# Strassen's seven products for part of the block pairs of the gates, mix_out and the down projection

## The chip, the cores and the metric

The kernel runs on one core of a Trainium2 chip. The metric is device time in microseconds (us): the median of three executions. One execution was recorded by the hardware profiler, and every row below comes from that one.

## The reference

One decoder layer for 256 tokens of width 2048, in float32. What matters here:

- `h = rms_norm(x)`, and `h @ w_in` gives q, k, v, the three inputs of a short convolution (1024 wide each) and two gates `ga`, `gc` (2048 wide each).
- `merged = sigmoid(ga) * (attention @ w_attn_out) + sigmoid(gc) * (convolution @ w_conv_out)`, and then `x = x + merged @ w_mix_out`.
- cross-attention to 256 memory tokens (`wkv_x`, `wq_x`, `wo_x`), and `u = relu(rms_norm(x) @ w_up)`, `x + (u * u) @ w_down` with a hidden width of 8192.
- a last `rms_norm`.

## The kernel before

**Three matmuls for each product.** Every matrix product runs as a sum of three in the type float32r: each operand is split into a high part (a copy rounded to float32r) and a low part (the rest), and hi x hi, hi x lo and lo x hi are added up in PSUM. The activations lie with the features on the partitions. Weights come from HBM in tiles of two 128-row blocks by 512 columns (512 KB, `load_w`, L58 on SP's queue, pool `wraw`, 6 buffers). `split_w` makes the high part on ScalarE (L66) and the low part on VectorE (L67), in pool `wsp`, 5 buffers each.

**Token groups.** `tok_group(w, c0, kr0, nk, xs, evac)` computes 512 columns for all 256 tokens: two PSUM banks, one for each half of the tokens, and for each of the nk 128-deep blocks and each half three 128x512 matmuls (L103 to L105). When a half is done, `evac` takes it out of PSUM. The up projection uses `feat_group` instead (L78 to L82), which puts its result by features.

**Stages in order.** q, k and v with the first group written out apart (it splits `x` and the weights as they land); self-attention and convolution, interleaved; then for each of four column blocks the two gates (L332 to L334, nk = 16, taken out by a ScalarE sigmoid straight from PSUM, L333), `w_attn_out` and `w_conv_out` (nk = 8, L337 to L342), and four pairs of transposes that put the merged block by features (`mg`); mix_out in four groups (L350 on, residual sum L355, sum of squares L189, transposes and `split_scaled`, L134 and L135, with `memory` for the memory tokens in between); cross-attention; and four times a quarter of the MLP, four up groups and four down groups (nk = 16, L459 adds to the residual). The last column block of the last down group is cut into half-width pieces, so that the end comes in small steps (L466, L510 to L520).

**Order of instructions.** The program text gives priorities; a scheduler at compile time lays out every engine's instructions by them and by a cost model of its own, so work written later can run earlier where its inputs are there by that model. Each engine then runs its own list strictly in order. The raw tile of `x` by tokens, `xtok`, is loaded at the start on ScalarE's DMA queue (L246), and the eight sums of squares for the first norm are ScalarE's (L189).

**PSUM.** Eight banks: five for accumulators (`mm`), three for transposes and attention (`aux`).

## Time and profile before

| what | value |
|---|---|
| median of 3 executions | 1476.53 us (1476.36 to 1476.88) |
| the profiled execution | 1476.77 us, span 1475.0 us |
| mean granted TensorE clock | 0.996 of 2.4 GHz |
| TensorE matmul busy | 1454.8 us (99%), 7064 matmuls |
| VectorE busy / ScalarE busy | 820.9 us (56%) / 691.2 us (47%) |
| HBM read | 277.98 MB, 190 GB/s over the span |

The span runs from the first to the last instruction; 1.77 us of the execution's time lie outside it. Busy times are unions of the records of an engine. A matmul's record is longer than the distance to the next one, since matmuls are pipelined, so TensorE's pace is read from start to start. The same holds in a smaller measure of VectorE and ScalarE.

### The profile page before, as it was taken

The page shows a single profiled execution, that of the slowest core. Times are in us where ns is not written, and L with a number is a line of the kernel's source. Part 1 is how long each engine was busy: PE and PEld are TensorE (multiplying, and loading weights), DVE is VectorE, ACT ScalarE, POOL GpSimd, SP SyncE. Part 2 cuts the span into 40 slices and gives each one's busy share as a digit, 9 for nine tenths or more (in the row PEclk, how much of TensorE's full clock was granted, in tenths as well). Part 3 has the DMA queues.
Part 4 walks back from the last instruction along what each step waited for, and adds up shares of the span by engine and source line. Part 5 has one row for each costly group of instructions (what it writes and reads, how often), then busy time and mean ns, then how long its engine had stood idle before and what let it go on. Part 6 is the DMA issues. An engine that isn't in the chain of part 4 may idle for free.

```text
span 1475.0 us, 18233 instructions
## 1 busy us (share of the span) xinstructions
PE 1454.8 (99%) x7064; PEld 1222.4 (83%) x7064; DVE 820.9 (56%) x976; ACT 691.2 (47%) x905; POOL 13.6 (1%) x21
## 2 busy tenths in 40 slices
PE   6999999999999999999999999999999999999997
PEld 5888888888888888888888888888888888888886
DVE  5545555765554646654476655556545555556554
ACT  6444544454444445554564443444434443445442
POOL 0000000000000000000000000000000000000011
PEclk9999999999999999999999999999999999999999
DMA  9666655576666667655555566565565556665652
GB/s 337 193 193 180 184 165 178 170 227 190 187 196 188 186 197 230 212 192 180 172 171 185 187 198 191 182 197 180 194 200 179 193 188 191 192 191 179 198 189 85
DMA packets 145158, 281.27 MB, mean 191 GB/s; under 512 B 8880, under 2 KB 9520, under 8 KB 144944
## 3 DMA queue, kind: packets, MB, share of 16 engines
q1 hardware_dynamic: 141888, 272.66, 58.9%
q10 hardware_dynamic: 3184, 7.45, 1.5%
q8 instruction: 55, 0.90, 0.2%
q14 instruction: 31, 0.25, 0.1%
HBM read 277.98 MB, written 2.10 MB: 190 GB/s over the span
## 4 chain that ended last, share of the span: by engine, by line
PE 98%; DMA 1%; ACT 1%; issue 0%; DVE 0%; POOLq 0%; POOL 0%; DVEq 0%; SPq 0%; ACTq 0%
PE acc L104 23%; PE acc L105 23%; PE acc L103 23%; PE acc L78 15%; PE acc L79 8%; PE aps L145 1%; PE acc L82 1%; DMA tok<-in_x_dram 1%; PE acc L81 1%; DMA raw<-in_w_in_dram 0%; ACT junk L189 0%; PE aps L315 0%; PE aps L270 0%; PE aps L438 0%; PE aps L407 0%
## 5 line engine op out<-in xcount | busy, mean ns | idle before, releaser
L67 DVE TENSOR_TENSOR wlo<-raw,whi 128x1024 fp32r<-128x1024 f32 (+1 forms) x510 | 618.7, 1222 | 561.2 <-ACT whi L66 547.5
L66 ACT ACTIVATE whi<-raw 128x1024 fp32r<-128x1024 f32 (+1 forms) x510 | 532.9, 1055 | 564.1 <-PE acc L105 386.2
L103 PE MATMUL acc<-whi,S 128*128 128x512 f32 x1512 | 584.9, 388 | 11.4 <-ACT whi L66 11.4
L105 PE MATMUL acc<-whi,S 128*128 128x512 f32 x1512 | 587.9, 389 | 0.0
L104 PE MATMUL acc<-wlo,S 128*128 128x512 f32 x1512 | 586.3, 388 | 0.3 <-DVE wlo L67 0.3
L103 PEld LDWEIGHTS acc<-whi,S 128*128 128x128 f32 x1512 | 284.6, 188 | 68.8 <-ACT whi L66 12.7
L78 PE MATMUL acc<-S,whi 128*128 128x512 f32 x960 | 341.6, 398 | 0.0
L104 PEld LDWEIGHTS acc<-wlo,S 128*128 128x128 f32 x1512 | 284.5, 188 | 58.8 <-DVE wlo L67 1.6
L105 PEld LDWEIGHTS acc<-whi,S 128*128 128x128 f32 x1512 | 284.7, 188 | 56.2
L79 PE MATMUL acc<-S,wlo 128*128 128x256 f32 x960 | 269.7, 281 | 0.0
L78 PEld LDWEIGHTS acc<-S,whi 128*128 128x128 f32 x960 | 180.4, 188 | 41.3
L79 PEld LDWEIGHTS acc<-S,wlo 128*128 128x128 f32 x960 | 181.3, 189 | 3.1
L474 ACT ACTIVATE blk<-acc 128x256 f32<-128x256 f32 x64 | 24.3, 380 | 36.0 <-PE acc L82 35.8
L189 ACT ACTIVATE junk<-tok 128x512 f32<-128x512 f32 (+1 forms) x33 | 20.2, 613 | 37.7 <-DVE tok L459 23.6
L459 DVE SCALAR_TENSOR_TENSOR tok<-acc,q,tok 128x512 f32<-128x512 f32 (+1 forms) x33 | 24.1, 731 | 18.0 <-PE acc L105 18.0
L130 ACT ACTIVATE S<-blk 128x512 fp32r<-128x512 f32 x32 | 20.0, 626 | 25.7 <-DVE blk L478 25.7
L475 DVE TENSOR_TENSOR blk<-acc,blk 128x256 f32<-128x256 f32 x64 | 27.0, 422 | 8.0 <-ACT blk L474 8.0
L131 DVE TENSOR_TENSOR S<-blk,S 128x512 fp32r<-128x512 f32 x32 | 22.1, 692 | 9.9 <-ACT S L130 8.4
L82 PE MATMUL acc<-S,whi 128*128 128x512 f32 x64 | 25.6, 400 | 0.0
L478 DVE SCALAR_TENSOR_TENSOR blk<-blk 128x512 f32<-128x512 f32 x32 | 22.0, 689 | 0.6
L204 ACT ACTIVATE blk<-acc,r 128x512 f32<-128x512 f32 x18 | 12.4, 689 | 15.5 <-PE acc L105 15.5
L81 PE MATMUL acc<-S,wlo 128*128 128x256 f32 x64 | 18.1, 283 | 0.0
(127 smaller groups left out, 466.2 us busy)
## 6 DMA issues: line engine op xcount, KB each, us to landing
raw<-in_w_in_dram SPq DMA_DIRECT2D x158, 512.0 KB, 4.2
raw<-in_w_up_dram SPq DMA_DIRECT2D x128, 512.0 KB, 4.0
raw<-in_w_down_dram SPq DMA_DIRECT2D x128, 512.0 KB, 4.3
raw<-in_w_mix_out_dram SPq DMA_DIRECT2D x32, 512.0 KB, 4.9
raw<-in_w_attn_out_dram SPq DMA_DIRECT2D x16, 512.0 KB, 4.3
raw<-in_w_conv_out_dram SPq DMA_DIRECT2D x16, 512.0 KB, 4.5
raw<-in_wkv_x_dram SPq DMA_DIRECT2D x16, 512.0 KB, 4.2
raw<-in_wq_x_dram SPq DMA_DIRECT2D x8, 512.0 KB, 3.9
```

The lines of the kernel that those rows point to most:

```text
L66: nc.scalar.activation(hi[:, k:k + step, :], raw[:, k:k + step, :], AF.Copy)
L67: nc.vector.tensor_sub(lo[:, k:k + step, :], raw[:, k:k + step, :], hi[:, k:k + step, :].bitcast(F32))
L78: nc.tensor.matmul(ps, a, xs(k, 2), start=(k == 0), stop=False)
L79: nc.tensor.matmul(ps[:, S:], c, xs(k, 0), start=False, stop=False)
L81: nc.tensor.matmul(ps[:, S:], c, xs(k, 0), start=False, stop=False)
L82: nc.tensor.matmul(ps, a, xs(k, 2), start=(k == 0), stop=True)
L103: nc.tensor.matmul(ps, xh, wh, start=(k == 0), stop=False)
L104: nc.tensor.matmul(ps, xh, wl, start=False, stop=False)
L105: nc.tensor.matmul(ps, xl, wh, start=False, stop=(k == nk - 1))
L459: nc.vector.scalar_tensor_tensor(t, ps, q3[:, h:h + 1], t, op0=ALU.mult, op1=ALU.add)
L474: nc.scalar.activation(z[:, b, :], ps[:, S:], AF.Copy)
L475: nc.vector.tensor_add(z[:, b, :], ps[:, :S], z[:, b, :])
```

## The change

A new function, `pair_group`, computes 1024 columns (two blocks of 512) for all tokens and takes the 128-deep blocks two at a time. A pair of depth blocks, the two token halves and the two column blocks make a 2 by 2 by 2 block product. A plain pair does its eight products (three matmuls each), a pair marked `True` does seven in the Winograd form of Strassen's scheme: four sums of weight blocks are formed (`weight_sums`, four VectorE subtractions of 128x512) and split like weights, four sums of activation blocks are formed once for each activation (`act_sums`), and the seven products go to seven PSUM banks, an eighth being used by plain pairs. At the end of a group `p1` is copied by ScalarE, four VectorE additions make `u2`, `u3`, `u4` and `v`, and each of the four output blocks is its bank plus one of these.

Of eight pairs, four take seven products in the gates and in mix_out (`MIXED`, `MIXED_HIGH`), three in the down projection (`THREE`). `w_attn_out`, `w_conv_out`, the up projection, attention and q, k, v keep their groups. The gates and the output blocks run by pairs of column blocks. `xtok`'s buffer now holds the gates (`sg`), and `x` is loaded into it a second time before mix_out, on SP's queue. Pools change: `wraw` 6 to 4, `wsp` 5 to 4, `mm` 5 to 6, `aux` 3 to 2. At the start, `xtok`'s load and the sums of squares are put behind the last weight split of the first group on ScalarE. The last column block is no longer cut.

The diff, cut to its core (the old gate, residual, down and tail code that is removed is shown above):

```diff
-    wraw = ctx.enter_context(tc.tile_pool(name="wraw", bufs=6))
-    wsp = ctx.enter_context(tc.tile_pool(name="wsp", bufs=5))
+    wraw = ctx.enter_context(tc.tile_pool(name="wraw", bufs=4))
+    wsp = ctx.enter_context(tc.tile_pool(name="wsp", bufs=4))
     blk = ctx.enter_context(tc.tile_pool(name="blk", bufs=3))
     tmp = ctx.enter_context(tc.tile_pool(name="tmp", bufs=2))
-    mm = ctx.enter_context(tc.tile_pool(name="mm", bufs=5, space=PSUM))
-    aux = ctx.enter_context(tc.tile_pool(name="aux", bufs=3, space=PSUM))
+    wone = ctx.enter_context(tc.tile_pool(name="wone", bufs=1))
+    wsum = ctx.enter_context(tc.tile_pool(name="wsum", bufs=2))
+    mm = ctx.enter_context(tc.tile_pool(name="mm", bufs=6, space=PSUM))
+    aux = ctx.enter_context(tc.tile_pool(name="aux", bufs=2, space=PSUM))
...
+    last_split = [None]
...
+            last_split[0] = nc.scalar.activation(hi[:, k:k + step, :], raw[:, k:k + step, :], AF.Copy)
...
+    def load_row(w, k, c0):
+        raw = wraw.tile([P, 2, 512], F32, name="raw")
+        nc.sync.dma_start(raw, w[k * P:(k + 1) * P, c0:c0 + 1024].rearrange("p (a c) -> p a c", a=2))
+        return raw
+    def split_one(raw):
+        hi = wone.tile([P, 512], F32R, name="ohi")
+        lo = wone.tile([P, 512], F32R, name="olo")
+        nc.scalar.activation(hi, raw, AF.Copy)
+        nc.vector.tensor_sub(lo, raw, hi.bitcast(F32))
+        return hi, lo
+    def weight_sums(r1_, r2_):
+        ta = wsum.tile([P, 2, 512], F32, name="tsum")
+        tb = wsum.tile([P, 2, 512], F32, name="tsum")
+        nc.vector.tensor_sub(ta[:, 0, :], r1_[:, 1, :], r1_[:, 0, :])
+        nc.vector.tensor_sub(ta[:, 1, :], r2_[:, 1, :], r1_[:, 1, :])
+        nc.vector.tensor_sub(tb[:, 0, :], r2_[:, 1, :], ta[:, 0, :])
+        nc.vector.tensor_sub(tb[:, 1, :], r2_[:, 0, :], tb[:, 0, :])
+        return ta, tb
+    def act_sums(dst, kk, z):
+        t = small("xsum", (P, 512))
+        s1, s2, s3, s4 = (t[:, i * P:(i + 1) * P] for i in range(4))
+        a11, a21, a12, a22 = z[:, 0, :P], z[:, 0, P:], z[:, 1, :P], z[:, 1, P:]
+        nc.vector.tensor_add(s1, a21, a22)
+        nc.vector.tensor_sub(s2, s1, a11)
+        nc.vector.tensor_sub(s3, a11, a21)
+        nc.vector.tensor_sub(s4, a12, s2)
+        split_act(dst, kk, t)
+    def pair_group(w, c0, kr0, nk, xs, xsum, order, evac):
+        bank = {}
+        last = {}
+        for pair, seven in order:
+            for q in (1, 2, 3, 5, 7, 6, 4) if seven else (2, 3, 4, 8):
+                last[q] = pair
+        def add(q, pair, a, b, first, final):
+            if q not in bank:
+                bank[q] = psum_aux() if q in (4, 8) else psum_mm()
+            first = first and pair == firsts[q]
+            final = final and pair == last[q]
+            (ah, al), (bh, bl) = a, b
+            nc.tensor.matmul(bank[q], ah, bh, start=first, stop=False)
+            nc.tensor.matmul(bank[q], ah, bl, start=False, stop=False)
+            nc.tensor.matmul(bank[q], al, bh, start=False, stop=final)
+        firsts = {}
+        for pair, seven in order:
+            for q in (1, 2, 3, 5, 7, 6, 4) if seven else (2, 3, 4, 8):
+                firsts.setdefault(q, pair)
+        for pair, seven in order:
+            k = 2 * pair
+            r = [load_row(w, kr0 + k + i, c0) for i in range(2)]
+            def act(i, h):
+                return tuple(xs(k + i, p)[:, h * P:(h + 1) * P] for p in range(2))
+            if seven:
+                ta, tb = weight_sums(*r)
+                b11 = split_one(r[0][:, 0, :])
+                b21, b22 = split_w(r[1])
+                t1, t3 = split_w(ta)
+                t2, t4 = split_w(tb)
+                s1, s2, s3, s4 = (tuple(xsum[:, pair % 4, p, i * P:(i + 1) * P] for p in range(2)) for i in range(4))
+                for q, a, b in ((1, act(0, 0), b11), (2, act(1, 0), b21), (3, s4, b22), (5, s1, t1), (7, s3, t3),
+                                (6, s2, t2), (4, act(1, 1), t4)):
+                    add(q, pair, a, b, True, True)
+            else:
+                b = [split_w(t) for t in r]
+                for q, h, j in ((2, 0, 0), (3, 0, 1), (4, 1, 0), (8, 1, 1)):
+                    for i in range(2):
+                        add(q, pair, act(i, h), b[i][j], i == 0, i == 1)
+        x, y, z = block(), block(), block()
+        p1, u2, u3, u4, v = x[:, 0, :], x[:, 1, :], y[:, 0, :], y[:, 1, :], z[:, 0, :]
+        nc.scalar.activation(p1, bank[1], AF.Copy)
+        nc.vector.tensor_add(u2, bank[6], p1)
+        nc.vector.tensor_add(u3, bank[7], u2)
+        nc.vector.tensor_add(u4, bank[5], u2)
+        nc.vector.tensor_add(v, bank[5], u3)
+        for q, h, j, u in ((2, 0, 0, p1), (3, 0, 1, u4), (4, 1, 0, u3), (8, 1, 1, v)):
+            evac(h, j, bank[q], u)
+    MIXED = [(0, True), (1, True), (4, False), (2, True), (5, False), (3, True), (6, False), (7, False)]
+    THREE = [(0, True), (3, False), (1, True), (4, False), (2, True), (5, False), (6, False), (7, False)]
+    MIXED_HIGH = [((p + 4) % 8, s) for p, s in MIXED]
...
+        tag = {"s": "ta", "xsum": "ta", "pT": "tb", "zm": "tb", "rsw": "tc", "y": "tc", "junk": "ta"}.get(name, name)
...
+    hS = big.tile([P, 4, 2, 512], F32R, name="SS")
+    def hsums():
+        for pair in range(4):
+            z = block()[:, 0, :].rearrange("p (k s) -> p k s", k=2)
+            for i in range(2):
+                k = 2 * pair + i
+                nc.vector.tensor_scalar(z[:, i, :], xraw[:, k, :], g_of(0, k), None, op0=ALU.mult)
+            act_sums(hS, pair, z)
...
-                    if q >= 4:
-                        o = (q - 4) * 512
-                        nc.scalar.dma_start(xtok[:, :, o:o + 512], xv[:, :, o:o + 512])
-                nc.scalar.dma_start(csb, rope)
                 sp = const.tile([P, 2, 4], F32, name="r1sp")
-                for h in range(2):
+                with tc.issue_after(last_split[0].ins):
+                    nc.scalar.dma_start(csb, rope)
                     for d in range(4):
-                        sumsq(sp[:, h, d:d + 1], xtok[:, h, d * 512:(d + 1) * 512], 512)
+                        nc.scalar.dma_start(xtok[:, :, d * 512:(d + 1) * 512], xv[:, :, d * 512:(d + 1) * 512])
+                    for d in range(4):
+                        for h in range(2):
+                            sumsq(sp[:, h, d:d + 1], xtok[:, h, d * 512:(d + 1) * 512], 512)
+                hsums()
...
-    for j in range(4):
-        sg = big.tile([P, 2, 2, 512], F32, name="R")
+    mS = None
+    for jp in range(2):
+        sg = big.tile([P, 2, 2, 1024], F32, name="tok")
         for i in range(2):
-            def ev_g(h, ps, i=i, sg=sg):
-                nc.scalar.activation(sg[:, i, h, :], ps, AF.Sigmoid, scale=r1[:, h:h + 1])
-            tok_group(w_in, 6 * AW + i * D + j * 512, 0, KD, hx, ev_g)
-        def ev_a(h, ps, sg=sg):
-            nc.vector.tensor_mul(sg[:, 0, h, :], ps, sg[:, 0, h, :])
-        tok_group(w_attn_out, j * 512, 0, 8, parts_of(acT), ev_a)
-        def ev_v(h, ps, sg=sg):
-            nc.vector.tensor_mul(sg[:, 1, h, :], ps, sg[:, 1, h, :])
-            nc.vector.tensor_add(sg[:, 0, h, :], sg[:, 0, h, :], sg[:, 1, h, :])
-        tok_group(w_conv_out, j * 512, 0, 8, parts_of(acT, 8), ev_v)
-        def ev_m(b, pt, j=j):
-            split_act(mg, 4 * j + b, pt.rearrange("p (k s) -> p k s", k=2), 2)
-        to_features(sg[:, 0, :, :], 0, 4, ev_m)
+            def ev_g(h, j, ps, u, i=i, sg=sg):
+                t = sg[:, i, h, j * 512:(j + 1) * 512]
+                nc.vector.tensor_add(t, ps, u)
+                nc.scalar.activation(t, t, AF.Sigmoid, scale=r1[:, h:h + 1])
+            pair_group(w_in, 6 * AW + i * D + jp * 1024, 0, KD, hx, hS, MIXED, ev_g)
...
+        if jp == 1:
+            mS = big.tile([P, 4, 2, 512], F32R, name="SS")
+        for c in range(2):
+            o = c * 512
+            def ev_a(h, ps, sg=sg, o=o):
+                nc.vector.tensor_mul(sg[:, 0, h, o:o + 512], ps, sg[:, 0, h, o:o + 512])
+            tok_group(w_attn_out, jp * 1024 + o, 0, 8, parts_of(acT), ev_a)
+            def ev_v(h, ps, sg=sg, o=o):
+                a, b = sg[:, 0, h, o:o + 512], sg[:, 1, h, o:o + 512]
+                nc.vector.tensor_mul(b, ps, b)
+                nc.vector.tensor_add(a, a, b)
+            tok_group(w_conv_out, jp * 1024 + o, 0, 8, parts_of(acT, 8), ev_v)
+            def ev_m(b, pt, jp=jp, c=c, mS=mS):
+                k = 8 * jp + 4 * c + b
+                z = pt.rearrange("p (k s) -> p k s", k=2)
+                if jp == 1:
+                    z = small("zm", (P, 2, S))
+                    nc.scalar.activation(z, pt.rearrange("p (k s) -> p k s", k=2), AF.Copy)
+                    act_sums(mS, k // 2 - 4, z)
+                split_act(mg, k, z, 2)
+            to_features(sg[:, 0, :, o:o + 512], 0, 4, ev_m)
+    xtok = big.tile([P, 2, D], F32, name="tok")
+    nc.sync.dma_start(xtok, xv)
+    def residual_pairs(w, xs, xsum, dst, gi, name, between):
...
+            def ev(h, j, ps, u, jp=jp):
+                c = 2 * jp + j
+                t = xtok[:, h, c * 512:(c + 1) * 512]
+                nc.vector.tensor_add(t, u, t)
+                nc.vector.tensor_add(t, ps, t)
+                sumsq(sp[:, h, c:c + 1], t, 512)
+            def ev_f(b, pt, jp=jp):
+                for i in range(2):
+                    k = 8 * jp + b + i
+                    split_scaled(dst, k, pt[:, i * S:(i + 1) * S], g_of(gi, k))
+            pair_group(w, jp * 1024, 0, KD, xs, xsum, MIXED_HIGH, ev)
+            to_features(xtok, 8 * jp, 8, ev_f)
+            between(2 * jp)
+            between(2 * jp + 1)
...
-    sp2 = residual(w_mix_out, KD, parts_of(mg), x2g, 1, "r2", memory)
+    sp2 = residual_pairs(w_mix_out, parts_of(mg), mS, x2g, 1, "r2", memory)
...
+    def add_down(h, o, ps, u):
+        t, r = xf_[:, h, o:o + 512], q3[:, h:h + 1]
+        nc.vector.scalar_tensor_tensor(t, u, r, t, op0=ALU.mult, op1=ALU.add)
+        nc.vector.scalar_tensor_tensor(t, ps, r, t, op0=ALU.mult, op1=ALU.add)
...
-    def add_last(h, ps, o, n, i, engine):
-        t = add_block(h, ps, o, n)
-        sumsq(ssf[:, h, i:i + 1], t, n)
-        engine.tensor_mul(t, t, gf[:, o:o + n])
...
+        uS = big.tile([P, 4, 2, 512], F32R, name="SS")
...
+                    if k < 6:
+                        act_sums(uS, k // 2, t)
...
+        for jp in range(2):
+            def ev_d(h, j, ps, u, jp=jp, g=g):
+                o = jp * 1024 + j * 512
+                t = add_down(h, o, ps, u)
+                if g == NG - 1:
+                    sumsq(ssf[:, h, 2 * jp + j:2 * jp + j + 1], t, 512)
+                    (nc.vector if jp else nc.gpsimd).tensor_mul(t, t, gf[:, o:o + 512])
+                    if jp and j:
+                        finish(h)
+            pair_group(w_down, jp * 1024, g * KG, KG, parts_of(uT), uS, THREE, ev_d)
```

## Rows read from the trace of the kernel before

**Rows 1.** The page: busy time, share and instructions of each engine.

```profile
PE 1454.8 (99%) x7064; PEld 1222.4 (83%) x7064; DVE 820.9 (56%) x976; ACT 691.2 (47%) x905; POOL 13.6 (1%) x21
```

**Rows 2.** Windows: busy time by engine, granted clock, DMA share, GB/s in five stretches.

```profile
core 0: us, PE busy (x) PEld busy (x) DVE busy (x) ACT busy (x) POOL busy (x), PEclk, DMA share, GB/s
0.00:37.00 37.00, 25.31 (x94) 19.12 (x95) 21.00 (x33) 25.86 (x49) 2.85 (x11) 0.91 0.96 337
...
438.20:504.40 66.20, 66.20 (x298) 54.78 (x296) 34.39 (x32) 29.10 (x30) 0.00 (x0) 1.00 0.63 191
...
571.00:660.00 89.00, 89.00 (x412) 73.75 (x410) 52.89 (x66) 53.09 (x87) 1.39 (x2) 1.00 0.66 214
...
757.00:846.10 89.10, 89.10 (x510) 77.55 (x509) 54.94 (x72) 42.46 (x61) 0.00 (x0) 1.00 0.58 187
846.10:933.20 87.10, 87.10 (x386) 72.14 (x385) 45.83 (x44) 35.19 (x35) 0.00 (x0) 1.00 0.61 194
```

**Rows 3.** Timeline, TensorE: two starts three matmuls apart, 512 and 256 columns wide.

```profile
600.15 0.39 PE L103 MATMUL acc<-whi,S 128*128 128x512 f32 x1
...
600.83 0.39 PE L103 MATMUL acc<-whi,S 128*128 128x512 f32 x1
...
1464.15 0.28 PE L103 MATMUL acc<-S,S 128*128 128x256 f32 x1
...
1464.51 0.28 PE L103 MATMUL acc<-S,S 128*128 128x256 f32 x1
```

**Rows 4.** Timeline, VectorE near the end: start, length; neighbours without a gap.

```profile
1439.18 1.23 DVE L67 TENSOR_TENSOR S<-raw,S 128x1024 fp32r<-128x1024 f32 x1 [1.09 <-ACT S L66]
1440.33 1.22 DVE L67 TENSOR_TENSOR wlo<-raw,whi 128x1024 fp32r<-128x1024 f32 x1
...
1444.41 0.74 DVE L459 SCALAR_TENSOR_TENSOR tok<-acc,q,tok 128x512 f32<-128x512 f32 x1
1445.07 1.22 DVE L67 TENSOR_TENSOR S<-raw,S 128x1024 fp32r<-128x1024 f32 x1
...
1462.36 0.69 DVE L466 TENSOR_TENSOR tok<-tok,S 128x512 f32<-128x512 f32 x1 [0.85 <-ACT junk L189]
1462.97 0.21 DVE L512 TENSOR_SCALAR rf<-ssf,pre 128x1 f32<-128x1 f32 x1
```

**Rows 5.** Timeline, VectorE in the first group: four in a row.

```profile
27.20 1.66 DVE L135 SCALAR_TENSOR_TENSOR S<-S,gcol,S 128x256 fp32r<-128x256 f32 x4
```

**Rows 6.** Groups by line and shape: count, busy us, mean ns, idle before.

```profile
L67 DVE TENSOR_TENSOR wlo<-raw,whi 128x1024 fp32r<-128x1024 f32 x506 | 616.0, 1226 | 555.3 <-ACT whi L66 541.5
...
L66 ACT ACTIVATE whi<-raw 128x1024 fp32r<-128x1024 f32 x506 | 530.5, 1058 | 563.0 <-PE acc L105 386.2 <-issue 131.5 <-PE acc L78 41.4
...
L135 DVE SCALAR_TENSOR_TENSOR S<-aps,gcol,S 128x256 fp32r<-128x256 f32 x32 | 14.0, 478 | 2.2 <-ACT S L134 1.9
```

**Rows 7.** Timeline, TensorE at the start: the first matmuls.

```profile
5.88 1.22 PE L103 MATMUL acc<-whi,S 128*128 128x512 f32 x2 [5.88 <-ACT whi L66]
...
7.32 0.63 PE L105 MATMUL acc<-whi,S 128*128 128x512 f32 x1
7.75 0.63 PE L104 MATMUL acc<-wlo,S 128*128 128x512 f32 x1
...
16.40 1.22 PE L103 MATMUL acc<-whi,S 128*128 128x512 f32 x2 [3.37 <-ACT whi L66]
```

**Rows 8.** The chain that ended last, at the start: start, length, what.

```profile
5.66 8.14 DMA tok<-in_x_dram
...
13.88 1.95 ACT junk L189 x6
```

**Rows 9.** Waits of SP's DMA queue: total us, times, longest.

```profile
SPq L58 <- DVE wlo L67: 1016.4, 431, 8.4
```

**Rows 10.** Timeline, GpSimd beside VectorE at the same moment.

```profile
1399.42 1.29 POOL L466 TENSOR_TENSOR tok<-tok,S 128x512 f32<-128x512 f32 x1 [741.41 <-ACT junk L189]
...
1400.34 1.46 DVE L67 TENSOR_TENSOR wlo<-raw,whi 128x1024 fp32r<-128x1024 f32 x1 [1.75 <-ACT whi L66]
```

**Rows 11.** Timeline, VectorE after the last matmul of the kernel.

```profile
1466.51 0.48 DVE L459 SCALAR_TENSOR_TENSOR tok<-acc,q,tok 128x256 f32<-128x256 f32 x1 [0.62 <-PE acc L105]
```

More of the change, by code (lines that the diff above doesn't have):

```diff
@@ L65, in split_w @@
         for k in range(0, nk, step):
-            nc.scalar.activation(hi[:, k:k + step, :], raw[:, k:k + step, :], AF.Copy)
+            last_split[0] = nc.scalar.activation(hi[:, k:k + step, :], raw[:, k:k + step, :], AF.Copy)
             nc.vector.tensor_sub(lo[:, k:k + step, :], raw[:, k:k + step, :], hi[:, k:k + step, :].bitcast(F32))
@@ L451, in hybrid_block @@
     nc.scalar.dma_start(gf, norm_final[None, :].to_broadcast([P, D]))
[L452 removed]
+    ssf = const.tile([P, 2, 4], F32, name="ssf")
     NG = 4
```

75 lines of the change are left out of this document (26 added, 49 removed).

## The prediction

> **What bounds the kernel now.** I read four views in this order. The page's busy times first [rows 1]: TensorE is busy 99% of the span, VectorE 56%. A share over the whole says nothing of one stage, so the windows come next [rows 2]: TensorE is busy in every microsecond of each of the four later stretches, at a granted clock of 1.00, and only the first 37 us have a gap. VectorE takes 34.4 of 66.2 us in one column block of the gates, 52.9 of 89.0 in mix_out, 54.9 of 89.1 in an up stage and 45.8 of 87.1 in a down stage. Then TensorE's pace from start to start [rows 3]: three 512-wide matmuls take 0.68 us, so one costs 0.2267 us, and a 256-wide one 0.12 us. A column block of the gates has 288 such matmuls and 8 transposes; 288 x 0.2267 = 65.3 us of the window's 66.2. So matmul count times 0.2267 is the time there, and a matmul less is 0.2267 us gained as long as its operands are ready. Last the waits: the high part of a weight split (L66) waits 386 us in all for a TensorE group to free its buffer [rows 6], so splits run ahead of TensorE and the buffers are full.
>
> VectorE's own pace decides whether this stays so. Neighbours without a gap [rows 4] start 1.15 us apart after a 128x1024 split, 0.61 after a 128x512 operation with two inputs, 0.66 after the three-operand one that reads PSUM. A 128x256 `split_scaled` takes (1.66 - 0.48) / 3 = 0.39 us [rows 5]. The recorded means are longer, 1.226 for the split [rows 6]; I keep them as the upper bound.
>
> **Matmuls removed.** A plain pair is 24 matmuls (5.44 us), a pair of seven 21 (4.76 us). Pairs of seven: four gate groups x 4, two mix_out groups x 4, eight down groups x 3, together 48, so 144 matmuls less: 144 x 0.2267 = 32.6 us. The last column block's 96 half-width matmuls (11.5 us) become 48 whole ones (10.9): 0.6 us. All weight loads go with their matmuls.
>
> **VectorE work added.** A plain pair costs VectorE two splits, 2.30 us. A pair of seven costs four weight sums, one half split and three whole ones: 5 x 0.61 + 3 x 1.15 = 6.50 us, against 4.76 us of TensorE. By groups:
>
> - gates: 4 x 6.50 + 4 x 2.30 + 8 additions at the end (4.9) = 40.1 us, TensorE 180 x 0.2267 = 40.8;
> - mix_out: the same splits, 12 additions (7.3), 8 `split_scaled` (3.1) and two calls of `memory` (3.1) = 48.7, TensorE 40.8 and 16 transposes;
> - down: 3 x 6.50 + 5 x 2.30 + 4 additions (2.4) + 8 three-operand ones (5.3) = 38.7, TensorE 41.5.
>
> Inside a group a seven and a plain pair alternate, 8.8 us of VectorE to 10.2 of TensorE: hidden. ScalarE is not the bound: at its recorded 1.06 us [rows 6] a seven needs 3.5 x 1.06 = 3.7 us. The buffers let a split run about one pair ahead, so what counts is each border between two groups, where the evacuation, the sums of the next sevens and the splits come together.
>
> - Gates, first group to second: from the end of the last seven to the next group's first plain pair TensorE has two plain pairs and two sevens, 20.4 us. VectorE has 2.3 (the last plain pair's splits) + 4.9 + 2 x 6.50 + 2.3 = 22.5. It is 2 us late, twice: 4 us. The border to `w_attn_out` has slack, since plain groups use half of VectorE.
> - mix_out, first to second: 22.5 + 2.4 (four more additions) + 3.1 (`split_scaled`), and 3.1 if `memory` falls there: 28.0 to 31.1 against 20.4. Late by 7.6 to 10.7; I take 9, and 1 more for the entry, where the activation sums of mix_out are made: 10 us.
> - Down, first to second: TensorE has three plain pairs and one seven, 21.1 us; VectorE 4.6 + 7.7 + 6.5 + 2.3 = 21.1. Even on paper; I take 0.7 each for buffers that come free late, four times: 3 us (0 to 8). Up to down and down to up are covered: up leaves 34 us of VectorE idle in 89 [rows 2], and the added activation sums take under 2 us per pair of blocks.
> - `aux` falls to two banks, which each pair group holds nearly throughout. At the border of convolution and gates transposes and the fourth product want the same two; I take 1 us (0 to 4). Attention has column groups beside it to fill its waits.
>
> Together 4 + 10 + 3 + 1 = 18 us given back. From below the bound is 0 (splits run ahead further than I count), from above the recorded lengths in place of the distances, worked out in the second rival.
>
> **The start.** TensorE begins at 5.9 us; at 7.3 us matmuls start 0.43 us apart, nearly twice 0.2267, which is the lower of its two clock levels (1.2 GHz, not 2.4), and at 16.4 us, after 3.4 us of idling, a pair of them is as slow as the first pair was [rows 7]. The granted clock of the window is 0.91 [rows 2]. The chain shows why: the load of `xtok` takes 8.1 us and six sums of squares stand in ScalarE's list ahead of the weight splits [rows 8]. The group's 96 matmuls need 21.8 us and are through at 37.0. The change puts load and sums behind the last split. What remains is 6.3 MB of `x` and weights, 18.7 us at the 337 GB/s of that window [rows 2], faster than TensorE uses them. With 12 matmuls at the slow pace, 5.9 + 12 x 0.43 + 84 x 0.2267 = 30.1, so at most 6.9 us are gained. The sums now wait in ScalarE's list for 2 MB that come later, with the second group's splits behind them, and the first norm is late next; a part may be lost there. I take 6 us (0 to 7). The eight scalings and the sums of `hsums` go where VectorE idles (16 of the first 37 us).
>
> **The end.** After the last matmul the addition reads 512 columns, not 256: 0.75 for 0.48 us [rows 4, 11], the sum of squares is longer by about as much, and a reduction joins the chain: +0.7 us (0 to 4, if VectorE is still busy with the other blocks).
>
> **GpSimd.** In the last down group's first half four GpSimd multiplies run among VectorE's two-input operations, where VectorE has little slack. The trace has that pairing: a multiply at 1399.42 for 1.29 us, and a split beginning at 1400.34 that took 1.46 us, not 1.23 [rows 10]. So 0.2 us each, under 1 us in all, taken as nothing. The Trainium skill (SBUF — State Buffer, section "Who interferes with whom") says more: such a VectorE operation and a GpSimd operation that reads SBUF shut each other out, the second blocked until the first is done. By that rule the split would have waited some 0.37 us longer than the trace leaves it, and the sum would be worse by up to the fourth rival's amount; the trace shows a stretch and no block.
>
> **The sum**, against the profiled execution: 1476.8 - 32.6 - 0.6 - 6 + 18 + 0.7 = 1456.3. The median is 0.2 below that execution, so 1456 us, 1.4% less.
>
> **Rivals.**
>
> 1. VectorE stays hidden. For it: splits wait 386 us for buffers today. Against: 48.7 of 42.6 in mix_out cannot be hidden. With no stalls 1476.8 - 33.2 - 6 + 0.7 = 1438; with 6 us in mix_out alone 1444.
> 2. VectorE becomes the bound of every pair group. If each operation costs its recorded length (1.226 and 0.69, 0.75, 0.48) because it waits for ScalarE's high part or for the sum before it, a gate group costs 43.9, mix_out 54.3, down 42.4. Two old column blocks took 43.5 (45.3 with transposes). Change: 4 x 0.4 + 2 x 9.0 - 8 x 1.1 = +10.8 in place of all that the matmuls gain, then -6 and +0.1 at the ends: 1482, slower. It decides from some 38 us of stalls on; at 30 to 38 the time is within 0.2%. For it: a split's low part does wait for the high one, 541 us in all [rows 6]. Against: those waits are idle time, and the neighbours of [rows 4] overlap.
> 3. `x`'s second load blocks SP. SP's queue is in order and today mostly waits for splits to free a raw tile [rows 9]. If the 2 MB load stands ahead of mix_out's weights while it waits for the gates' last transposes, those weights start late: 6.2 to 9.8 us for the transfer (337 or 214 GB/s [rows 2]) and 2.3 for a split, less what was loaded ahead. 7 to 12 us more: 1463 to 1468.
> 4. GpSimd locks VectorE out: four multiplies of 1.3 us in a stage without slack, 5 us: 1461. This is the rule named above; the trace speaks against it.
> 5. The start gains nothing, because the sums of squares block ScalarE again: 1462.
>
> **How the numbers follow.** Chances: the forecast 53% (1447 to 1465), rival one 12%, two 13%, three 9%, four 2%, five 11%. The likeliest's 1456 is the prediction. From 1439 to 1473 leaves out rival two (13%) and the part of rival one below 1439 (some 5%): 18%. About 0.2%, 3 us, is what a measurement can tell from no change. Rival two is slower in 9 of its 13%, and within 0.2% in the other 4, where only part of it comes; all others are faster: 87%, 4%, 9%.
>
> **What would show it.** In the profile after: some 190 matmul records fewer than now (144, and 48 of the cut block); first group's matmuls through near 31 us; one pair group of the down projection near 42 us and one of the gates between 41 and 43; VectorE busy over 90% in mix_out, and TensorE's largest idle sum there, waiting for L67's split or the weight sums, at the start of the second mix_out group. A group that TensorE runs without idling, or gaps that wait for a DMA or a PSUM bank instead, would show a step wrong. The prediction fails if VectorE's lists come in another order than the needs, so that sevens wait in the middle of groups, not at their borders.

## The result, and the profile after

The changed kernel is slower: 1495.27 us (1491.47 to 1497.46), against 1476.68 for the kernel before on the same chip, a ratio of 1.0123 [1.0099, 1.0148]. The prediction was 1456. The profiled execution took 1491.47 us, with a span of 1489.7; it is the fastest of the four, so the rows below account for 14.7 of the 18.6 us by which the median rose.

In the rows below, L70 and L71 are the high and low parts of a weight split (L66 and L67 before), L124 the load of one row of a pair (`load_row`), L130 and L131 the half split (`split_one`), L138 to L141 the weight sums, L169 to L171 the three matmuls of one product, L608 and L609 the down projection's additions. The page's busy times answer to [rows 1]:

```profile
PE 1442.3 (97%) x6872; PEld 1190.2 (80%) x6872; DVE 1105.0 (74%) x1482; ACT 778.1 (52%) x1037; POOL 14.5 (1%) x19
```

192 matmuls are gone, as forecast, and VectorE has 284 us more. TensorE's share fell from 99% to 97% of a longer span: it idles. The windows show where, one for each kind of stage; they answer to [rows 2]:

```profile
core 0: us, PE busy (x) PEld busy (x) DVE busy (x) ACT busy (x) POOL busy (x), PEclk, DMA share, GB/s
0.00:37.00 37.00, 30.64 (x123) 24.07 (x124) 21.93 (x36) 23.77 (x42) 1.59 (x10) 1.00 0.91 310
293.00:386.00 93.00, 86.89 (x373) 68.60 (x372) 82.57 (x109) 52.47 (x61) 0.00 (x0) 0.98 0.56 177
431.50:515.80 84.30, 83.36 (x367) 67.38 (x366) 76.60 (x92) 49.79 (x55) 0.00 (x0) 1.00 0.60 194
561.60:661.00 99.40, 89.83 (x379) 69.36 (x378) 91.84 (x128) 59.55 (x89) 0.00 (x0) 0.97 0.63 211
764.00:857.00 93.00, 93.00 (x540) 81.29 (x539) 63.31 (x92) 47.60 (x71) 0.00 (x0) 1.00 0.59 183
...
856.90:942.70 85.80, 84.56 (x365) 67.48 (x364) 76.97 (x93) 44.69 (x52) 0.00 (x0) 1.00 0.61 193
```

The start (first row) has a granted clock of 1.00, not 0.91, and 123 matmuls where there were 94. The two gate stages, mix_out and down (second, third, fourth and last row) leave TensorE idle; an up stage (fifth) does not. In mix_out, VectorE is busy 92% and the granted clock falls to 0.97.

To size this I took, for every matmul, the distance from its start to the next one's, less the pace of its width (0.2267 us for 512 columns, 0.12 for 256), and summed what was left over. The borders between the stages are drawn by hand and remainders under 0.1 us hardly count, so a part is good to about half a microsecond. The table gives the change from before to after of each part:

| part | predicted, us | measured, us |
|---|---|---|
| matmuls | -33.2 | -33.2 |
| start, first 60 us | -6 | -4.2 |
| gates, with their entry | +4 +1 | +11.9 |
| mix_out | +10 | +16.3 |
| after mix_out | 0 | +1.8 |
| down | +3 | +16.6 |
| from the last matmul's start to the end | +0.7 | +4.9 |
| sum | -20.5 | +14.1 (the span: +14.7) |

The saving came in full. The parts from the gates to down lose 46.6 us (idling, and slow matmuls behind it) where 18 were allowed. The largest miss is the down projection, and there VectorE stands still too. This is one gap of the second down stage in the timeline (start, length, what; in brackets the idle time before and what ended it), VectorE's, ScalarE's and TensorE's rows together:

```profile
1044.24 2.35 DVE L71 TENSOR_TENSOR wlo<-tsum,whi 128x1024 fp32r<-128x1024 f32 x2
1048.13 0.69 DVE L131 TENSOR_TENSOR olo<-raw,ohi 128x512 fp32r<-128x512 f32 x1 [1.54 <-ACT ohi L130]
...
1047.47 0.63 ACT L130 ACTIVATE ohi<-raw 128x512 fp32r<-128x512 f32 x1 [3.71 <-DMA raw<-in_w_down_dram]
...
1046.03 0.39 PE L169 MATMUL aps<-whi,S 128*128 128x512 f32 x1
1048.16 0.50 PE L169 MATMUL acc<-ohi,S 128*128 128x512 f32 x1 [1.74 <-ACT ohi L130]
```

ScalarE stands 3.71 us before a half split whose load has not landed; VectorE idles 1.54 us behind it and TensorE 1.74. This is one kind of gap: between 840 and 1450 us TensorE waits 2.8 us for half splits and 5.4 for VectorE's splits. The chain that ended last goes through the same moment and says why the load is late (start, length, what):

```profile
1033.64 0.60 DVE tsum L138
...
1038.96 0.68 DVE tsum L140
...
1040.85 1.15 DVE wlo L71
...
1042.01 5.44 DMA raw<-in_w_down_dram
...
1047.47 0.64 ACT ohi L130
...
1048.16 0.50 PE acc L169
```

The weight sums of one seven begin at 1033.6 and stand in VectorE's list among the up stage's last work; a split that reads a raw tile ends at 1042.0; by this chain only that frees the tile for the next load, which takes 5.4 us. The page's list of loads has 4.6 as the median (last column):

```profile
raw<-in_w_down_dram SPq DMA_DIRECT2D x128, 512.0 KB, 4.6
```

The waits over the whole span (total us, times, longest) say the same. First the compute engines':

```profile
ACT ohi L130 <- DMA raw<-in_w_down_dram: 61.8, 19, 5.5
...
DVE tsum L138 <- DMA raw<-in_w_down_dram: 26.2, 12, 3.3
```

Before, the waits of a split for these loads came to 4.3 us; it was TensorE that splits waited for [rows 6]. Then those of SP's queue, for a raw tile to come free:

```profile
SPq L124 <- DVE wlo L71: 299.2, 146, 10.9
SPq L124 <- DVE tsum L139: 166.8, 42, 8.1
SPq L124 <- DVE tsum L141: 68.8, 27, 8.9
```

### The profile page after: what moved, and what is told of

Same layout as the page of the kernel before. It is cut to its first block, busy times and chain, and to the rows that moved or that the text cites. A ratio compares the mean times of both kernels' runs of the same rounds, so it can differ in the third digit from the quotient of the medians.

```text
span 1489.7 us, 18544 instructions
## 1 busy us (share of the span) xinstructions
PE 1442.3 (97%) x6872; PEld 1190.2 (80%) x6872; DVE 1105.0 (74%) x1482; ACT 778.1 (52%) x1037; POOL 14.5 (1%) x19
## 4 chain that ended last, share of the span: by engine, by line
PE 67%; DVE 15%; DMA 12%; issue 3%; ACT 3%; ACTq 0%; SPq 0%; DVEq 0%; POOL 0%
PE acc L82 13%; PE acc L108 8%; PE acc L109 8%; PE acc L107 8%; PE acc L83 6%; DVE wlo L71 6%; DMA raw<-in_w_down_dram 6%; PE acc L170 4%; PE acc L171 4%; PE acc L169 4%; PE aps L170 3%; PE aps L171 3%; PE aps L169 2%; DMA raw<-in_w_in_dram 2%; DMA raw<-in_w_mix_out_dram 2%
## 5 line engine op out<-in xcount | busy, mean ns | idle before, releaser
L71 DVE TENSOR_TENSOR wlo<-raw,whi 128x1024 fp32r<-128x1024 f32 (+1 forms) x466 | 562.6, 1219 | 251.7 <-ACT whi L70 246.0
L70 ACT ACTIVATE whi<-raw 128x1024 fp32r<-128x1024 f32 (+1 forms) x466 | 481.6, 1052 | 348.3 <-PE acc L109 109.3
L107 PE MATMUL acc<-whi,S 128*128 128x512 f32 (+1 forms) x624 | 238.3, 390 | 5.9 <-ACT whi L70 5.9
L108 PE MATMUL acc<-wlo,S 128*128 128x512 f32 (+1 forms) x624 | 242.2, 389 | 1.7 <-DVE wlo L71 1.7
L109 PE MATMUL acc<-whi,S 128*128 128x512 f32 (+1 forms) x624 | 241.4, 388 | 0.0
L70 ACT ACTIVATE whi<-tsum 128x1024 fp32r<-128x1024 f32 x96 | 101.4, 1057 | 93.3 <-DVE tsum L141 42.7
L107 PEld LDWEIGHTS acc<-whi,S 128*128 128x128 f32 x624 | 117.5, 189 | 29.6 <-ACT whi L70 6.7
L108 PEld LDWEIGHTS acc<-wlo,S 128*128 128x128 f32 x624 | 117.7, 189 | 26.9 <-DVE wlo L71 4.2
L109 PEld LDWEIGHTS acc<-whi,S 128*128 128x128 f32 x624 | 117.6, 188 | 22.7
L170 PE MATMUL acc<-wlo,S 128*128 128x512 f32 x304 | 121.1, 398 | 7.9 <-DVE wlo L71 7.7
L71 DVE TENSOR_TENSOR wlo<-tsum,whi 128x1024 fp32r<-128x1024 f32 x96 | 116.5, 1219 | 6.1 <-ACT whi L70 5.3
L171 PE MATMUL acc<-whi,S 128*128 128x512 f32 x304 | 119.2, 392 | 0.0
L170 PE MATMUL aps<-wlo,S 128*128 128x512 f32 x304 | 119.0, 392 | 0.0
L171 PE MATMUL aps<-whi,S 128*128 128x512 f32 x304 | 118.2, 391 | 0.0
L169 PE MATMUL aps<-whi,S 128*128 128x512 f32 x304 | 111.4, 393 | 2.3 <-DVE y L429 1.3
L169 PE MATMUL acc<-whi,S 128*128 128x512 f32 x304 | 109.3, 395 | 0.9 <-ACT whi L70 0.6
L170 PEld LDWEIGHTS acc<-wlo,S 128*128 128x128 f32 x304 | 57.4, 189 | 26.0 <-DVE wlo L71 14.2
```

The source lines that it names most:

```text
L70: last_split[0] = nc.scalar.activation(hi[:, k:k + step, :], raw[:, k:k + step, :], AF.Copy)
L71: nc.vector.tensor_sub(lo[:, k:k + step, :], raw[:, k:k + step, :], hi[:, k:k + step, :].bitcast(F32))
L107: nc.tensor.matmul(ps, xh, wh, start=(k == 0), stop=False)
L108: nc.tensor.matmul(ps, xh, wl, start=False, stop=False)
L109: nc.tensor.matmul(ps, xl, wh, start=False, stop=(k == nk - 1))
L169: nc.tensor.matmul(bank[q], ah, bh, start=first, stop=False)
```

## The experiments

Two explanations of the lost time stood against each other: loads come late, because the change cut the raw tiles from six to four and a seven holds its tiles longer; or VectorE has too much to do at the borders between pair groups. The first four kernels were built on the changed kernel (the first on the one before), the next four on the kernel with six raw tiles, the last four as said. Each ran beside the kernel before on the same chip, 1476.5 to 1476.75 us.

**The new start alone**, in the kernel before: loads of `x` and the sums of squares behind the last split.

```diff
...
-                    if q >= 4:
...
-                        nc.scalar.dma_start(xtok[:, :, o:o + 512], xv[:, :, o:o + 512])
...
+                with tc.issue_after(last_split[0].ins):
...
+                    for d in range(4):
+                        nc.scalar.dma_start(xtok[:, :, d * 512:(d + 1) * 512], xv[:, :, d * 512:(d + 1) * 512])
...
```

> The kernel before with one edit of the change alone: the load of x by tokens and its sums of squares behind the last weight split of the first group. In the changed kernel TensorE lost about 5 us less in its first 20 us than before (9.3 us of gaps and slow matmuls against 4.3). If that is the start edit's own doing, this kernel takes 1476.7 - 5 = 1471 to 1472 us; if the gain belongs to the smaller pools or to the longer lead of other work, it stays within 1 us of 1476.7.

1470.22 us, 0.9956 of the time of the kernel before [0.9942, 0.9971] (such a ratio and its 95% interval stand behind every time below): 6.5 us gained. The start's term was right; in the changed kernel two of its microseconds are lost again between 40 and 60 us, a gap that six raw tiles remove.

**Six raw tiles.** To make room, `xo` takes the place of the activation sums, which are not alive then.

```diff
-    wraw = ctx.enter_context(tc.tile_pool(name="wraw", bufs=4))
+    wraw = ctx.enter_context(tc.tile_pool(name="wraw", bufs=6))
...
-    xo = big.tile([P, NX, 2, S], F32R, name="R")
+    xo = big.tile([P, NX, 2, S], F32R, name="SS")
```

> The changed kernel with six raw weight tiles in place of four (room made by giving xo the buffer of the activation sums, which is free then). Load theory: a pair of seven holds its two raw tiles until the last weight sum, so the next loads start late and their 4 to 5 us of latency show; VectorE and ScalarE wait some 100 us in all for raw tiles of w_down, and two more tiles hide that: 10 to 15 us less than 1495, the down stages at 84 us or less. VectorE theory: the borders are short of VectorE time, not of tiles; within 3 us of the changed kernel.

1468.17 us, 0.9934 [0.9918, 0.9951]: 27.1 us less than the changed kernel, about twice what was expected, and faster than the one before. In the profiled executions it is 21.6 us, some 16 of them in down. All VectorE's work is still there. The first down stage in the windows, to be held against the last row of those above:

```profile
850.60:933.60 83.00, 83.00 (x366) 68.42 (x365) 74.45 (x89) 44.23 (x49) 0.00 (x0) 1.00 0.62 199
```

TensorE does not idle, with 366 x 0.2267 = 83.0 us. The wait of the half split for its load, 61.8 us above, is

```profile
ACT ohi L130 <- DMA raw<-in_w_down_dram: 7.4, 5, 1.7
```

**Without the weight sums.** It leaves the weight sums out: the splits that read them read the raw tiles. Four raw tiles remain.

```diff
-                ta, tb = weight_sums(*r)
...
-                t1, t3 = split_w(ta)
-                t2, t4 = split_w(tb)
+                t1, t3 = split_w(r[0])
+                t2, t4 = split_w(r[1])
```

> The changed kernel without the four weight sums of each pair of seven: their splits read the raw tiles instead. It leaves out part of the computation. VectorE does 2.4 us less in each of 48 pairs (117 us), and raw tiles are held longer than in the changed kernel, since the late splits read them. VectorE theory: most of the 45 us of stalls goes, 1460 to 1470 us. Load theory: the tiles are as late as before or later, within 8 us of 1495.

1461.07 us, 0.9896 [0.9881, 0.9911]. The windows at the place of the changed kernel's first down stage:

```profile
856.90:942.70 85.80, 85.80 (x403) 71.56 (x402) 61.26 (x66) 41.70 (x44) 0.00 (x0) 1.00 0.64 205
```

The time came out where the VectorE theory had put it, not the load theory, though this run takes 105 us of work from VectorE. TensorE does not idle in down (the window takes in some of an up stage here; over all of 820 to 1450 us the gaps are 1.4 us more than before the change), and yet loads are still late there:

```profile
ACT ohi L130 <- DMA raw<-in_w_down_dram: 45.6, 18, 6.0
ACT whi L70 <- DMA raw<-in_w_down_dram: 28.6, 25, 3.6
```

So late loads alone do not stall down, and by the run with six tiles VectorE's work alone does not either. The loss takes both: loads that come late from four tiles, and a VectorE that has too little slack to make up for it.

**All pairs plain**, in the same column pairs, with four raw tiles. Sums, extra additions and the splits of sums go with the sevens.

```diff
...
+    MIXED = [(p, False) for p, s in MIXED]
+    THREE = [(p, False) for p, s in THREE]
...
```

> The changed kernel with every pair plain: same groups of 1024 columns, same pools, banks, start and end, no products of seven, no sums. TensorE has 33 us of matmuls more than in the changed kernel, VectorE far less. If the new frame is free but for the end (5 us longer) and the start (5 us shorter), 1476 us. If the frame itself stalls TensorE (two transposing banks held by each group, four raw tiles), 1482 to 1490, and then the sevens are not the only cost.

1488.74 us, 1.0084 [1.0069, 1.0099]. Without a single seven the new frame (column pairs, four raw tiles, two `aux` banks) loses: it has 48 matmuls less than the kernel before and still takes 12 us more. There are no gaps in down, but 8.9 us at the border inside mix_out, 3.7 more at the gates' entry than before, and 3.6 after the last matmul. The timeline at the mix_out border (L240 and L241 are the high and low parts of `split_scaled` in this kernel):

```profile
617.54 0.51 ACT L240 ACTIVATE S<-blk,gcol 128x256 fp32r<-128x256 f32 x1 [4.13 <-DMA blk<-in_memf_dram]
...
621.08 0.77 PE L169 MATMUL aps<-whi,S 128*128 128x512 f32 x1 [6.37 <-DVE S L241]
```

ScalarE works in order and stands 4.13 us before a split of memory tokens whose load is late; transposed blocks queue behind it, and with two `aux` banks the fourth product can't begin.

**The transposes of both halves after mix_out** (six raw tiles):

```diff
...
-            to_features(xtok, 8 * jp, 8, ev_f)
+            evs.append(ev_f)
+            if jp == 1:
+                for i in range(2):
+                    to_features(xtok, 8 * i, 8, evs[i])
```

> The kernel with six raw tiles, and in mix_out all transposes of the new residual behind the second group, so none stands at the border of the two groups. That kernel loses 14 us at 560 to 640 us, most of it at that border, and the all-plain one loses 9 there with VectorE half idle, its fourth product waiting 6.4 us for a transposing bank. Bank theory: 1468 - 8 = 1460, border under 5 us. VectorE theory (sums, splits and evacuation at once): 1465 to 1468.

1463.86 us, 0.9915 [0.9900, 0.9930], 4 us better than six raw tiles alone, with intervals that overlap: a little better than the VectorE theory's range, short of the bank theory's 1460. The gaps of mix_out as a whole shrink only from 14.3 to 12.2 us.

**The end of the kernel before** for the last half (six raw tiles): one whole column block, then the cut one with its two 256-wide pieces.

```diff
-            pair_group(w_down, jp * 1024, g * KG, KG, parts_of(uT), uS, THREE, ev_d)
+            if g < NG - 1 or jp == 0:
+                pair_group(w_down, jp * 1024, g * KG, KG, parts_of(uT), uS, THREE, ev_d)
...
+    tok_group(w_down, 1024, (NG - 1) * KG, KG, parts_of(uT), lambda h, ps: add_last(h, ps, 1024, 512, 2, nc.gpsimd))
...
```

> The kernel with six raw tiles, and the last 1024 columns of the last down group as before the change (a plain group, then the block cut into halves). It gives back three pairs of seven (2.0 us) and 0.6 us of half-width matmuls. From the last matmul's start to the end it took 13.7 us, before the change 8.8. If the bunched evacuation of four banks is the cause of the late end, the end takes 9 us again and the time is 1468 - 4.9 + 2.6 = 1466. If the end stays at 13 us, it is the output's own DMA, and the time is 1471.

1466.04 us, 0.9930 [0.9914, 0.9947]. From the last matmul's start to the end it takes 8.8 us, as before the change, against 13.7; the sevens and the half-width matmuls give back about half of that. Why 13.7, the changed kernel's timeline shows:

```profile
1476.02 0.39 PE L171 MATMUL aps<-whi,S 128*128 128x512 f32 x1
...
1474.63 1.41 DVE L609 SCALAR_TENSOR_TENSOR tok<-acc,q,tok 128x512 f32<-128x512 f32 x2 [5.53 <-PE acc L171]
1475.96 0.74 DVE L609 SCALAR_TENSOR_TENSOR tok<-aps,q,tok 128x512 f32<-128x512 f32 x1
...
1480.55 2.47 DVE L624 TENSOR_SCALAR tok<-tok,rf 128x512 f32<-128x512 f32 x6 [0.41 <-POOL rf L618]
```

The last pairs' products are interleaved over four banks, so all four finish within 2 us: four additions, four multiplies and VectorE's six scalings stand there together, not one block's.

**The first gate's group by single column blocks** (six raw tiles):

```diff
+            if i == jp == 0:
+                for j in range(2):
...
+                    tok_group(w_in, 6 * AW + j * 512, 0, KD, hx, ev_s)
+                continue
             pair_group(w_in, 6 * AW + i * D + jp * 1024, 0, KD, hx, hS, MIXED, ev_g)
```

> The kernel with six raw tiles, and the first of the four gate groups done by two plain groups, which hold no transposing bank beside the convolution's last transposes. It gives back 2.7 us of matmuls and one border. If the 8 us lost at 300 to 320 us come from those banks and the convolution's VectorE chain behind them, they go: 1468 - 8 + 3 = 1463. If the loss moves to the next gate group, 1470.

1461.67 us, 0.9904 [0.9890, 0.9919]: 6.5 us less than six raw tiles alone, with 12 matmuls more. The entry of the gates in the changed kernel's timeline:

```profile
310.37 0.49 PE L169 MATMUL acc<-ohi,S 128*128 128x512 f32 x1 [1.66 <-ACT ohi L130]
...
313.08 0.77 PE L169 MATMUL aps<-whi,S 128*128 128x512 f32 x1 [1.26 <-DVE y L429]
```

and the same stretch of the variant in the windows:

```profile
290.00:325.00 35.00, 35.00 (x164) 29.05 (x163) 25.52 (x38) 18.00 (x22) 0.00 (x0) 1.00 0.60 180
```

In the changed kernel the second wait is that of a product for an `aux` bank, which the convolution's last work on VectorE (L429) still holds. The first is a split that is late beside that work. A plain group takes away the sums as well as the banks, so this run does not part them; the all-plain kernel, without any sums, lost 3.7 us here.

**Memory loads into raw tiles** in place of the shared blocks (six raw tiles):

```diff
-        m = block().rearrange("p a (b s) -> p (a b) s", s=S)
+        m = wraw.tile([P, 2, 512], F32, name="raw").rearrange("p a (b s) -> p (a b) s", s=S)
...
-        mt = block()
+        mt = wraw.tile([P, 2, 512], F32, name="raw")
```

> The kernel with six raw tiles, and the memory tokens loaded into raw weight tiles, not into the three blocks that a pair group's evacuation takes. In the all-plain kernel ScalarE waits 4.1 us for such a load with the transposed features' splits behind it, and TensorE waits for the bank that they hold. Load theory: these loads come earlier, the border in mix_out loses 5 to 8 us less, 1460 to 1463 us. Bank and VectorE theories: no change, 1468.

1467.41 us, 0.9937 [0.9923, 0.9952]: nothing that can be measured. The edit did what it was for: between 575 and 625 us ScalarE waits 1.1 us for the loads by features, with six raw tiles alone 4.3. So the late memory load is not what limits mix_out by itself.

**Mix_out by single column blocks too**, together with the old end and the plain first gate (six raw tiles):

```diff
...
-    sp2 = residual_pairs(w_mix_out, parts_of(mg), mS, x2g, 1, "r2", memory)
+    sp2 = residual(w_mix_out, KD, parts_of(mg), x2g, 1, "r2", memory)
...
```

> Six raw tiles, the first gate group plain, the old end, and mix_out as before the change (four plain groups, no activation sums for it). It gives back 5.4 us of matmuls for mix_out on top of the 2.7 and 2.6 of the other two. VectorE theory for mix_out (96% busy at the border in the two runs that moved transposes and memory loads): all of its 17 us of stalls go, and with 9 us of end the time is 1461.7 + 5.4 - 17 - 4.9 + 2.6 = 1448. If the stalls came from what stands around mix_out (the gates' end, the memory tokens), some 8 of them stay, 1456.

1450.08 us (1448.38 to 1451.12), 0.9820 [0.9806, 0.9835]: faster than both kernels, and near the VectorE theory's 1448. This run changes three places at once. Mix_out in the changed kernel and here, by the windows:

```profile
590.00:622.00 32.00, 26.14 (x107) 19.80 (x106) 29.77 (x44) 19.70 (x36) 0.00 (x0) 0.91 0.69 226
```

```profile
560.00:660.00 100.00, 100.00 (x458) 82.77 (x457) 59.05 (x72) 57.77 (x93) 1.39 (x2) 1.00 0.69 227
```

At the border TensorE was busy 26.1 of 32 us at a granted clock of 0.91, with VectorE at 93%; here it does not idle at all.

**No multiplies on GpSimd** (six raw tiles): the four of the last group's first half on VectorE.

```diff
-                    (nc.vector if jp else nc.gpsimd).tensor_mul(t, t, gf[:, o:o + 512])
+                    nc.vector.tensor_mul(t, t, gf[:, o:o + 512])
```

> The kernel with six raw tiles, and the four multiplications of the last down group's first half on VectorE, not on GpSimd. In the changed kernel VectorE's two-input operations beside them took 1.12 to 1.14 us, not 0.69. If that contention stalls TensorE, the 1.5 us of gaps near 1430 us go, and at most 2 us of time. If VectorE's own 4 x 0.61 us cost as much, no change from 1468.

1469.09 us, 0.9942 [0.9924, 0.9960], against 1468.17: the same. The gap near 1430 us (1.26 us with six raw tiles) is gone from the trace, but a gain of that size cannot be told in these times.

**Four sevens in the down groups**, on the version of 1450 us:

```diff
...
+    THREE = [(0, True), (4, False), (1, True), (5, False), (2, True), (6, False), (3, True), (7, False)]
...
-                    if k < 6:
+                    if k < 8:
```

> The kernel with mix_out plain, and four pairs of seven in place of three in each remaining down group, alternating with plain ones. Seven groups save 0.68 us more each, 4.8 us. VectorE then has 4 x 6.5 + 4 x 2.3 + 7.7 = 42.9 us in a group of 40.8. VectorE theory: each group now stalls by 2 to 4 us, 5 to 15 us slower than that kernel. If loads alone set the pace, 4 us faster.

1454.78 us (1451.79 to 1456.69), 0.9851 [0.9837, 0.9866]: 4.7 us slower, just short of the 5 to 15 expected, though 21 matmuls (4.8 us) are gone. A group now asks 42.9 us of VectorE (4 x 6.50 + 4 x 2.30 + 2.4 + 5.3) for 180 x 0.2267 = 40.8 of TensorE. The windows over 600 us, this run and the one with three sevens:

```profile
840.00:1440.00 600.00, 593.21 (x2981) 500.55 (x2980) 492.61 (x625) 310.66 (x376) 10.80 (x7) 1.00 0.60 188
```

```profile
840.00:1440.00 600.00, 598.36 (x3026) 507.37 (x3024) 462.45 (x576) 297.39 (x362) 12.12 (x7) 1.00 0.60 189
```

TensorE's idle time grows from 1.6 to 6.8 us. Of its waits 3.9 us, in three, are now for banks that VectorE's last additions have not emptied. With enough raw tiles VectorE is the limit, and three sevens of eight pairs stay on the right side of it.

**Five raw tiles**, `xo` moved as with six:

```diff
-    wraw = ctx.enter_context(tc.tile_pool(name="wraw", bufs=4))
+    wraw = ctx.enter_context(tc.tile_pool(name="wraw", bufs=5))
...
```

> The changed kernel with five raw tiles. Load theory: between four (1495) and six (1468) tiles, 1475 to 1485; VectorE's and ScalarE's waits for raw tiles of w_down (100 us with four) fall to under half. If one more tile is enough for a pair of seven, 1468 already.

1477.12 us, 1.0008 [0.9998, 1.0017]. Four, five and six tiles give 1495, 1477 and 1468. The time lies in the load theory's range. The half split's wait, though, did not fall to under half of its 61.8 us:

```profile
ACT ohi L130 <- DMA raw<-in_w_down_dram: 50.1, 19, 5.2
```

but ScalarE's wait now seldom reaches TensorE: 5 us of gaps are left in down, where there were 16.6. A wait is a loss only where it is longer than the work that is ready ahead of it.

## Why the prediction was wrong

The step that failed is the sentence "The buffers let a split run about one pair ahead, so what counts is each border between two groups", and with it the term "Down, first to second ... Even on paper; I take 0.7 each for buffers that come free late, four times: 3 us (0 to 8)". The argument had the order of VectorE's work and its price, but no price for a load. The diff takes the raw pool from six tiles to four; a pair needs two; a seven holds its tiles until its sums are done; a load takes 4.6 us. The lead is gone inside the groups, not only at their borders. The prediction had named the sign itself: gaps that wait for a DMA would show a step wrong. Down measured 16.6 us, outside the bound of 8, and two tiles more were worth 27.1 of the 39.3 us by which the median was missed. The waits for raw tiles [rows 9] were used for the third rival only, not to ask what two tiles fewer would do. Late loads are one of two causes, the sums' VectorE time the other: without the weight sums loads are late, too, and down does not idle. The kernels with five and six tiles also have `xo` elsewhere; that move was not run alone, but from five to six only the count changes, and 9 us go.

Point by point:

- **The matmuls**: 192 fewer, 33.2 us; right, and the pace of [rows 3] held.
- **VectorE's prices**: right. The sums start 0.60 us apart and the splits 1.14 where nothing interferes, and the run with four sevens falls behind where the sum of these prices says so.
- **Gates**: 11.9 us for 4 and 1. With six raw tiles 9 remain, about 7 at the entry. The term mis-sized is the `aux` one, 1 us with a bound of 4: there the two banks, the convolution's last work on VectorE and the first sums meet. In the kernels without weight sums and without any seven 2.1 and 3.7 us are lost there, so the rest goes with the sums.
- **Mix_out**: 16.3 for 10, 14.3 with six raw tiles. The place and VectorE's share (over 90%) were right, but VectorE does not do it alone. Without the weight sums 13.2 us of gaps are left there, and 8.9 appear without any seven. In the run without sums VectorE is busy only 24.6 us from 580 to 612 us, and TensorE waits for ScalarE all the same; the changed kernel has that wait, too. First the run without sums, then the changed kernel:

```profile
602.09 1.22 PE L169 MATMUL acc<-whi,SS 128*128 128x512 f32 x2 [4.74 <-ACT whi L70]
```

```profile
617.64 0.80 PE L169 MATMUL acc<-whi,SS 128*128 128x512 f32 x1 [3.26 <-ACT whi L70]
```

In both, the chain that ended last comes from a load of memory tokens, through their splits and the sums of squares in ScalarE's list, to this weight split. "ScalarE is not the bound" held for its work, not for its order. With the memory loads in raw tiles no wait there is over 1.1 us, but VectorE is busy 31.0 of 32 us, many short waits for its splits take the place, and the sum stays. So two causes lie over each other, and taking one away leaves the other. Only going back to single column blocks removed the idling. The banks' share stays open: their number and that of the split buffers (`wsp`) were not varied alone.
- **Down**: above. The rival that makes VectorE the bound of every pair group had the sign and nearly the size, 1482, but not the cause: with six raw tiles all its work fits under TensorE in the first three down stages, 83.3 us each from the first down matmul to the next up one, for 83.0 of matmuls.
- **The start**: -4.2 in place, -6.5 alone, for 6. The sums of squares do not block the splits, so the fifth rival fell.
- **The end**: 4.9 for 0.7. I costed the last block's addition and took the other blocks as done, with their work only in the bound of 4. The order of the last products makes all four finish together.
- **`x`'s second load**: the third rival came, at a small part of its price of 7 to 12 us. SP waited 6.0 us for the gates' last work before this load, with mix_out's weights behind it. The weight load issued next took 8.5 us, the chain that ended last goes through it, and TensorE lost about 1 us to splits that were late for it. With six raw tiles that load takes 10.7 us and TensorE waits 1.2. First SP's wait, then TensorE's with six raw tiles:

```profile
SPq L473 <- DVE tok L458: 6.0, 1, 6.0
```

```profile
575.97 0.51 PE L169 MATMUL acc<-ohi,S 128*128 128x512 f32 x1 [1.16 <-ACT ohi L130]
```

- **GpSimd**: taken as nothing. Its multiplies do lock VectorE out, as the fourth rival says (last section). Behind them stands the longest wait of TensorE in down: 2.76 us in the changed kernel, where VectorE had also lost 1.40 us to a late load, 1.26 with six raw tiles, none without the multiplies. The rival's 5 us did not come.

The mechanism of the first rival, VectorE hidden, is what the 1450 us version reaches nearly everywhere: the sevens that it keeps pay, and they stand where little other work runs beside TensorE's.

## What to carry to other kernels

When a change pays for new tiles by shrinking a pool, price the pool first: the time a tile is held, plus the time of its load, against the number of tiles times the consumer's pace for one. Work that fits under the bound engine as a sum over a group can still stall it, since in-order engines and a few banks make it wait for the latest of several things at each border; convert one stage at a time and keep those whose TensorE row shows no idling. Here the stages without other work beside them gained, and the crowded ones were better left as they were.

## What the hardware did that I had not expected

GpSimd shuts VectorE out more nearly than I had said. These are the four multiplies of the last down group, from the timeline of the changed kernel, first GpSimd's, then VectorE's operations beside them:

```profile
1431.83 1.46 POOL L650 TENSOR_TENSOR tok<-tok,S 128x512 f32<-128x512 f32 x1 [754.29 <-ACT junk L289]
1433.63 1.38 POOL L650 TENSOR_TENSOR tok<-tok,S 128x512 f32<-128x512 f32 x1 [0.33 <-ACT junk L289]
1435.40 1.31 POOL L650 TENSOR_TENSOR tok<-tok,S 128x512 f32<-128x512 f32 x1 [0.40 <-ACT junk L289]
1437.11 1.28 POOL L650 TENSOR_TENSOR tok<-tok,S 128x512 f32<-128x512 f32 x1 [0.40 <-ACT junk L289]
...
1432.71 1.14 DVE L131 TENSOR_TENSOR olo<-raw,ohi 128x512 fp32r<-128x512 f32 x1
1433.77 0.74 DVE L609 SCALAR_TENSOR_TENSOR tok<-aps,q,tok 128x512 f32<-128x512 f32 x1
1434.43 1.12 DVE L139 TENSOR_TENSOR tsum<-raw 128x512 f32<-128x512 f32 x1
...
1436.14 1.12 DVE L140 TENSOR_TENSOR tsum<-raw,tsum 128x512 f32<-128x512 f32 x1
1437.19 3.42 DVE L71 TENSOR_TENSOR wlo<-raw,whi 128x1024 fp32r<-128x1024 f32 x2
```

Where a multiply had 0.58, 0.58, 0.57 and 1.20 us left when VectorE's two-input operation began, that operation took 0.45, 0.43, 0.43 and 1.07 us longer than undisturbed (0.69; 2.35 for the two splits): each time what was left, less some 0.13 us. The row of [rows 10] fits as well, 0.37 left and 0.23 longer: a split that was blocked for the whole 0.37 would have been only 0.14 us longer than that row, not 0.37 as the prediction has it. The addition that takes one input from PSUM (L609) ran in its usual 0.74 us inside a multiply. The Trainium skill (SBUF — State Buffer, section "Who interferes with whom") says both: two inputs from SBUF contend, one does not. These rows agree with it; my reading of one row as a stretch without a block was too coarse. The price is 2.4 us of VectorE for the four, and TensorE stands behind the first of the two splits:

```profile
1439.53 0.79 PE L170 MATMUL acc<-wlo,S 128*128 128x512 f32 x1 [2.76 <-DVE wlo L71]
```

Moving the multiplies to VectorE, with six raw tiles, changed the time by nothing that can be measured.
